# New prices in a kernel's planner, and the low part of a key copied by ScalarE

## The chip, the core and the metric

The kernel runs on one core of a Trainium2 chip. The metric is the device time of one execution in microseconds (us). Names: PE is TensorE (matmuls), PEld its weight loads, DVE is VectorE, ACT is ScalarE, POOL is GpSimd, SP is SyncE, which issues most of the transfers.

## The reference

Two layers of an encoder trunk on x of 512 tokens by 1024, all in float32. Each layer computes

```
u = rms_norm(h)
proj = u @ w_in                        # 1024 x 7424: inputs of three mixers, and gates
a = differential_attention(...)        # 4 heads, two softmax maps each
r = bidirectional_retention(...)       # 4 heads, chunks of 128
c = grouped_query_attention(...)       # 8 query heads, 2 key heads
h = h + (sum over n of gate_n * (branch_n @ w_branch_n)) @ w_out
h = h + relu(rms_norm(h) @ w_mlp_in)**2 @ w_mlp_out      # 1024 -> 4096 -> 1024
```

## The kernel before

**Products.** A float32 operand is held as two tiles: a high part (`w_hi`, `dkh`, `xh`: a copy in the type fp32r, made by ACT) and a low part (`w_lo`, `dkl`, `xl`: the operand minus its high part, made by DVE). A product is three matmuls: high by high, high by low, low by high (`passes`). A matmul writes 128 rows by 512 or 256 columns. Weights come as 512 KB tiles `stage` (two buffers) through SP's queue and are split into `w_hi` and `w_lo` (six buffers). The pairs of MLP and gate units (`pair`, tiles `x`, `c`, `pu`) and the wide MLP products (`wide_product`, tiles `wide`, `A`, `wp`) use Strassen-like schemes: sums and differences on DVE, seven products in place of eight. In a pair, one PSUM tile serves several products in turn, and ACT must copy its content (`c<-x`, `pu<-x`) before the next product may write it.

**Stages of a layer.** Projections and retention come first (`rv`, `rq`, `rk`, `rg`, tiles `rsc`, `rav`), then the differential heads (`diff_head`; `qk` is normalised and rotated by a chain of POOL instructions, `qtr` is its transpose on PE, `dsc` the scores, `dav` the values), the grouped-query heads (`gsc`, `gav`), gates and branch projections, the output product `wo`, and the MLP (`x`, `wide`, `w`).

**The order is planned.** Nothing is issued while the program is written: every instruction goes into a list (`Plan.note`), with the instructions it depends on and a price in ns from `price()`. `Plan.order` then plays the list through: at each moment every idle engine takes, of the instructions whose inputs are ready and whose buffers are free, the one that stands earliest in the program, and is busy for its price. A result reaches another engine after a fixed time (`HOPS`, by pair of engines) plus 200 ns (`HOP`); a transfer through SP has its size by 360 bytes per ns and then 2000 ns. The sequence that comes out is the order in which each engine's instructions are issued. The chip's engines keep that order: an instruction that waits holds up everything behind it on its engine. So a price never changes what is computed, only the places.

Prices before, in ns, with n the columns:

```
matmul, fp32r                 2.5 + n / 2.4
ScalarE                       0.833 * n + 50 (PSUM) or 95
VectorE                       1.04 * n + 69
GpSimd power / other          300 + 165 * n  /  2.1 * n + 130
```

None of them looks at how many of the 128 partitions an instruction covers. Instructions on 64 partitions are those that shift half a tile to the other half: `sw` of `ev_rope_t`, `dq`, `gq`, `dkh`, `dkl`, `gkh`, `gkl` of `stack_q` and `stack_k`, `ctmp` of `gqa_head`.

**A key.** `stack_k` (line 1051) takes the transposed keys of two maps or heads from PSUM. For each of the two it fills all 128 partitions of `hi` and `lo` with the same 64 rows: ACT copies them twice, into their own half and into the other, and DVE subtracts twice. It is called once per differential head and once per layer for the grouped-query keys, each time for two keys: (4 + 1) x 2 x 2 layers = 20 keys.

Of the kernel before, what the change touches and what calls it, by code (L numbers as in the profile page):

```python
# [14 lines left out]
ALU = mybir.AluOpType  # L15
# [233 lines left out]
def free(x):  # L249
    return math.prod(x.shape[1:])  # L250


def price(engine, op, k):

    out = k["out"]
    n = free(out)
    if engine == "tensor":
        if op == "transpose":
            return 112
        if k["rhs"].tile.dtype == F32R:  # L260
            return 2.5 + n / 2.4 * (1 if n >= 256 else 4)
        return 195 if n == 1 else 4 * (2.5 + max(n, 128) / 2.4)
    src = k.get("in_", k.get("in0"))
    if src is not None:
        n = max(n, free(src))
    psum = any(isinstance(x, Ref) and x.tile.psum for x in k.values())
    if engine == "scalar":
        extra = 95 if isinstance(k.get("scale"), Ref) or isinstance(k.get("bias"), Ref) else 0
        return 0.833 * n + (50 if psum else 95) + extra + (100 if "accum_out" in k else 0)
    if engine == "vector":  # L270
        if op == "reciprocal":
            return 65 + 8 * n
        fast = op in ("tensor_scalar", "tensor_copy") and not psum
        pointer = any(isinstance(k.get(x), Ref) for x in ("scalar", "scalar1", "scalar2"))
        return (0.52 if fast else 1.04) * n + 69 + (61 if pointer else 0)
    if engine == "gpsimd":
        if k.get("op") == ALU.pow:
            return 300 + 165 * n
        return (3.4 if op in ("tensor_scalar", "tensor_copy") else 2.1) * n + 130
    return 700  # L280


# [5 lines left out]
class Plan:  # L288
# [16 lines left out]
    def note(self, engine, name, args, kwargs):  # L305
# [22 lines left out]
        for r in ins + outs:  # L328
            if r.tile not in seen:
                seen.append(r.tile)  # L330
                r.tile.users += 1
                if r.tile.first is None:
                    r.tile.first = i
                    o.new.append(r.tile)
        o.tiles = seen
        o.cost = price(engine, name, kwargs) if engine != "sync" else self.dma_price(kwargs)
        o.late = self.LATENCY.get(engine, 0.0)
        if engine == "gpsimd" and name == "dma_start":
# [133 lines left out]
class Core:  # L472
# [578 lines left out]
    def stack_k(self, srcs, nm):  # L1051

        p = self.turned(srcs)
        out = []
        for i in range(2):
            own = slice(i * 64, i * 64 + 64)
            hi, lo = self.g(nm + "h", F32R), self.g(nm + "l", F32R)
            for j in (i, 1 - i):
                self.nc.scalar.copy(out=hi[j * 64:j * 64 + 64], in_=p[own])
            for j in range(2):  # L1060
                self.nc.vector.tensor_tensor(out=lo[j * 64:j * 64 + 64], in0=p[own], in1=hi[own], op=ALU.subtract)
            out.append((hi, lo))
        return out

# [641 lines left out]
```

## Time and profile before

| | |
|---|---|
| median of 3 runs | 1773.45 us (1772.24 to 1774.34) |
| the profiled execution | 1772.2 us, of which its span 1770.4 us |
| busy, share of the span | PE 99%, weight loads 86%, DVE 84%, ACT 64%, POOL 19% |
| instructions | PE 10136, DVE 2438, ACT 2064, POOL 350 |
| granted clock of TensorE | 1.000 |
| moved by DMA | 201.95 MB, mean 114 GB/s |

The span runs from the first to the last instruction; busy time is what the instructions of an engine cover together. The ends of matmuls are modelled, so that the time from one start to the next tells more of PE than its busy share.

### The profile page before, as it was taken

What the parts mean: (1) busy time and instruction counts of PE and PEld (TensorE: products, weight loads), DVE (VectorE), ACT (ScalarE), POOL (GpSimd) and SP (SyncE); (2) the same over time, 40 slices, a digit from 0 to 9 for tenths busy, and PEclk for the clock granted to TensorE, in tenths of its full rate; (3) what the DMA queues carried; (4) which work ended last, traced back from release to release, by engine and by line L of the source; (5) the groups of instructions that cost most, each with busy time, mean ns of one, the idle gap of its engine ahead of it and who ended that gap; (6) DMA issues with size and microseconds to landing.
All of it is one profiled execution on the core that took longest, in us unless ns stands there. A gap on an engine that the chain in (4) does not pass through costs nothing.

```text
span 1770.4 us, 27228 instructions
## 1 busy us (share of the span) xinstructions
PE 1744.6 (99%) x10136; PEld 1525.3 (86%) x10136; DVE 1484.3 (84%) x2438; ACT 1139.0 (64%) x2064; POOL 339.9 (19%) x350
## 2 busy tenths in 40 slices
PE   8999999999999999999999999999999999999999
PEld 6887888889988989988888778888899899989887
DVE  7866887899978999999866667978999789998994
ACT  5544666785556877777535456768855568777771
POOL 2334463001110001111013235700012100011110
PEclk9999999999999999999999999999999999999999
DMA  6311212112355354747622122111124542646482
GB/s 205 106 61 48 86 66 72 48 48 73 115 183 179 96 178 103 219 96 225 206 93 71 48 76 68 60 60 60 36 97 133 160 172 92 211 99 182 96 249 84
DMA packets 76741, 201.95 MB, mean 114 GB/s; under 512 B 8896, under 2 KB 9408, under 8 KB 76608
## 3 DMA queue, kind: packets, MB, share of 16 engines
q1 hardware_dynamic: 68544, 185.53, 32.0%
q0 software_dynamic: 8064, 14.68, 5.6%
q8 instruction: 79, 1.29, 0.3%
q14 instruction: 54, 0.44, 0.1%
HBM read 169.77 MB, written 30.41 MB: 113 GB/s over the span
## 4 chain that ended last, share of the span: by engine, by line
PE 73%; DVE 11%; DMA 6%; ACT 5%; issue 3%; POOL 2%; SPq 0%; ACTq 0%; DVEq 0%; POOLq 0%
PE x L455 19%; PE wide L455 7%; PE proj L455 6%; PE gate L455 6%; DMA stage<-in_w 6%; PE w L455 5%; PE wo L455 5%; PE c L455 4%; DVE w_lo L461 4%; PE wtr L457 2%; PE rg L455 2%; PE gsc L455 2%; PE gav L455 2%; PE dsc L455 2%; PE rq L455 1%
## 5 line engine op out<-in xcount | busy, mean ns | idle before, releaser
L461 ACT CAST w_hi<-stage 128x1024 fp32r<-128x1024 f32 (+1 forms) x235 | 226.8, 968 | 169.0 <-DMA stage<-in_w 95.4
L461 DVE TENSOR_TENSOR w_lo<-stage,w_hi 128x1024 fp32r<-128x1024 f32 (+1 forms) x235 | 282.0, 1202 | 35.1 <-ACT w_hi L461 31.9
L455 PE MATMUL x<-u,w_hi 128*128 128x256 f32 x1472 | 276.1, 283 | 0.0
L455 PEld LDWEIGHTS x<-u,w_hi 128*128 128x128 f32 x1472 | 233.5, 192 | 2.5
L455 PE MATMUL x<-u,w_lo 128*128 128x256 f32 x736 | 208.3, 283 | 0.0
L461 POOL DMA_DIRECT2D sums<-wp x56 | 49.1, 876 | 560.1 <-ACT xh L461 475.2
L455 PEld LDWEIGHTS x<-u,w_lo 128*128 128x128 f32 x736 | 141.1, 192 | 0.0
L455 PE MATMUL wide<-w_lo,xh 128*128 128x512 f32 x336 | 130.9, 390 | 0.0
L455 PE MATMUL wide<-w_hi,xl 128*128 128x512 f32 x336 | 130.8, 389 | 0.0
L455 PE MATMUL wide<-w_hi,xh 128*128 128x512 f32 x336 | 129.7, 390 | 0.0
L461 DVE TENSOR_TENSOR w_lo<-A,w_hi 128x512 fp32r<-128x512 f32 x168 | 112.3, 684 | 10.3 <-ACT w_hi L461 9.5
L455 PE MATMUL x<-t23h,w_hi 128*128 128x256 f32 x368 | 105.2, 287 | 3.3 <-ACT c L461 3.0
L461 ACT CAST w_hi<-A 128x512 fp32r<-128x512 f32 x168 | 102.2, 621 | 8.2 <-ACT w_hi L461 2.7
L455 PE MATMUL gate<-u,w_hi 128*128 128x512 f32 x320 | 106.4, 399 | 0.0
L461 ACT ACTIVATE c<-c 128x512 f32<-128x512 f32 x156 | 94.0, 628 | 19.0 <-DVE c L461 17.3
L455 PE MATMUL x<-t23h,w_lo 128*128 128x256 f32 x368 | 104.3, 283 | 0.3 <-DVE w_lo L461 0.2
L455 PE MATMUL x<-t23l,w_hi 128*128 128x256 f32 x368 | 104.1, 283 | 0.0
L455 PE MATMUL c<-w_hi,u 128*128 128x512 f32 x256 | 86.1, 394 | 0.0
L455 PEld LDWEIGHTS x<-t23h,w_hi 128*128 128x128 f32 x368 | 70.3, 191 | 5.9 <-ACT c L461 5.3
L461 POOL TENSOR_TENSOR gth<-gth,c 128x512 f32<-128x512 f32 x28 | 40.8, 1465 | 178.1 <-DVE c L461 178.0
L455 PEld LDWEIGHTS wide<-w_hi,xl 128*128 128x128 f32 x336 | 63.1, 188 | 13.1
L455 PEld LDWEIGHTS wide<-w_lo,xh 128*128 128x128 f32 x336 | 63.1, 188 | 12.5
(299 smaller groups left out, 5208.9 us busy)
## 6 DMA issues: line engine op xcount, KB each, us to landing
stage<-in_w SPq DMA_DIRECT2D x235, 512.0 KB, 3.6
A<-in_w SPq DMA_DIRECT2D x96, 256.0 KB, 4.6
sums<-wp POOLq DMA_DIRECT2D x56, 256.0 KB, 6.0
sums<-wp SPq DMA_DIRECT2D x28, 256.0 KB, 2.8
wp<-sums SPq DMA_DIRECT2D x28, 256.0 KB, 4.7
h<-in_x SPq DMA_DIRECT2D x16, 256.0 KB, 4.4
mid<-h SPq DMA_DIRECT2D x16, 256.0 KB, 2.1
h<-mid SPq DMA_DIRECT2D x16, 256.0 KB, 6.3
```

The costliest lines, as they stand in the source:

```text
L455: self.nc.tensor.matmul(k.pop("out"), **k)
L457: self.nc.tensor.transpose(k["out"], k["in_"], k["identity"])
L461: getattr(getattr(self.nc, o.engine), o.name)(**k)
```

## The change

The prices of fp32r matmuls, of instructions on fewer than 128 partitions and of GpSimd become larger; and in `stack_k` the second subtraction becomes a copy by ACT of the first one's result.

```diff
         if k["rhs"].tile.dtype == F32R:
-            return 2.5 + n / 2.4 * (1 if n >= 256 else 4)
+            return 13.7 + n / 2.4 * (1 if n >= 256 else 4)
...
     if engine == "scalar":
-        return 0.833 * n + (50 if psum else 95) + extra + (100 if "accum_out" in k else 0)
+        shifted = 115 if out.shape[0] < 128 else 0
+        return 0.833 * n + (50 if psum else 95) + extra + (100 if "accum_out" in k else 0) + shifted
     if engine == "vector":
...
-        return (0.52 if fast else 1.04) * n + 69 + (61 if pointer else 0)
+        return (0.52 if fast else 1.04) * n + 69 + (61 if pointer else 0) + (115 if out.shape[0] < 128 else 0)
     if engine == "gpsimd":
         if k.get("op") == ALU.pow:
-            return 300 + 165 * n
-        return (3.4 if op in ("tensor_scalar", "tensor_copy") else 2.1) * n + 130
+            return 400 + 165 * n
+        return (3.4 if op in ("tensor_scalar", "tensor_copy") else 2.1) * n + 290
...
             hi, lo = self.g(nm + "h", F32R), self.g(nm + "l", F32R)
-            for j in (i, 1 - i):
-                self.nc.scalar.copy(out=hi[j * 64:j * 64 + 64], in_=p[own])
-            for j in range(2):
-                self.nc.vector.tensor_tensor(out=lo[j * 64:j * 64 + 64], in0=p[own], in1=hi[own], op=ALU.subtract)
+            other = slice(64 - i * 64, 128 - i * 64)
+            self.nc.scalar.copy(out=hi[own], in_=p[own])
+            self.nc.scalar.copy(out=hi[other], in_=p[own])
+            self.nc.vector.tensor_tensor(out=lo[own], in0=p[own], in1=hi[own], op=ALU.subtract)
+            self.nc.scalar.copy(out=lo[other], in_=lo[own])
```

The order moves nearly everywhere, by small steps. Three places follow.

PE in the first differential head of layer 1: the score matmuls (`dsc`) among the value projection (`dv`). Before:

```order
L455 MATMUL dsc<-dkh,dq 128x512
L455 MATMUL dv<-w_hi,u_250 128x512
L455 MATMUL dv<-w_lo,u_250 128x512
L455 MATMUL dv<-w_hi,u_278 128x512
L455 MATMUL dsc<-dkh,dq 128x512
L455 MATMUL dv<-w_hi,u_136 128x512
L455 MATMUL dv<-w_lo,u_136 128x512
L455 MATMUL dsc<-dkl,dq 128x512
```

Now:

```order
L456 MATMUL dsc<-dkh,dq 128x512
L456 MATMUL dv<-w_lo,u_146 128x512
L456 MATMUL dv<-w_hi,u_160 128x512
L456 MATMUL dv<-w_hi,u_170 128x512
L456 MATMUL dv<-w_lo,u_170 128x512
L456 MATMUL dv<-w_hi,u_184 128x512
L456 MATMUL dsc<-dkh,dq 128x512
L456 MATMUL dv<-w_hi,u_193 128x512
L456 MATMUL dv<-w_lo,u_193 128x512
L456 MATMUL dv<-w_hi,u_212 128x512
L456 MATMUL dv<-w_hi,u_202 128x512
L456 MATMUL dsc<-dkl,dq 128x512
```

Five projection matmuls now stand between the two that need the high parts, where there were three, and four before the first that needs a low part, where there were two.

DVE in the retention stage of layer 2: the low part of the last chunk's scores (`sdl`) and a weight's low part (`w_lo`). Before:

```order
L461 SCALAR_TENSOR_TENSOR sd<-rsc,decay 128x512 x3
L461 TENSOR_TENSOR sdl<-sd,sdh 128x512 x3
L461 SCALAR_TENSOR_TENSOR sd<-rsc,decay 128x512
L461 TENSOR_TENSOR rot<-rq,t_ret 128x512
L461 TENSOR_SCALAR decay<-delta,dec 128x896
L461 TENSOR_TENSOR w_lo<-stage,w_hi 128x1024
L461 TENSOR_TENSOR sdl<-sd,sdh 128x512
```

Now:

```order
L462 SCALAR_TENSOR_TENSOR sd<-rsc,decay 128x512 x2
L462 TENSOR_TENSOR sdl<-sd,sdh 128x512 x2
L462 SCALAR_TENSOR_TENSOR sd<-rsc,decay 128x512 x2
L462 TENSOR_SCALAR decay<-delta,dec 128x896
L462 TENSOR_TENSOR sdl<-sd,sdh 128x512 x2
L462 SCALAR_TENSOR_TENSOR decay<-delta,dec,decay 128x896
L462 TENSOR_TENSOR rot<-rq,t_ret 128x512
L462 TENSOR_TENSOR w_lo<-stage,w_hi 128x1024
```

The last `sdl` had `rot`, one `decay` instruction and `w_lo` ahead of it; `rot` and `w_lo` now stand behind it.

ACT in the MLP of layer 2, at the end of a wide product: the copies of the wide PSUM tiles (`wp`), the cast of a weight that comes by DMA (`w_hi<-stage`), and the copy `c<-x` that frees a pair's PSUM tile. Before:

```order
L461 COPY wp<-wide_17828 128x512
L461 CAST xh<-c_17437 128x256
L461 CAST xh<-c_17693 128x256
L461 COPY wp<-wide_17843 128x512
L461 CAST w_hi<-stage 128x1024
L461 COPY pu<-x_17886 128x256
L461 COPY c_17933<-x_17907 128x256
```

Now:

```order
L462 COPY wp<-wide_17802 128x512
L462 CAST w_hi<-stage 128x512
L462 CAST w_hi<-stage 128x1024
L462 COPY wp<-wide_17818 128x512
L462 CAST w_hi<-sa 128x1024
L462 COPY wp<-wide_17858 128x512
L462 CAST w_hi<-sb 128x1024
L462 COPY wp<-wide_17876 128x512
L462 COPY pu<-x_17915 128x256
L462 COPY c_17957<-x_17934 128x256
```

The casts of this pair's weights, which stood right ahead of `pu` and `c` or behind them, now stand ahead of three copies of wide tiles.

## Rows read from the trace of the kernel before

**Rows 1.** The page, part 1: busy us, share of the span, instructions.

```profile
PE 1744.6 (99%) x10136; PEld 1525.3 (86%) x10136; DVE 1484.3 (84%) x2438; ACT 1139.0 (64%) x2064; POOL 339.9 (19%) x350
```

**Rows 2.** The chain that ended last, 590 to 640 us: start, length, what.

```profile
610.03 10.07 PE x L455 x84
620.11 10.91 PE wide L455 x48
```

**Rows 3.** Waits of PE's matmuls: us in total, times, longest.

```profile
PE x L455 <- ACT c L461: 5.8, 9, 1.1
PE dsc L455 <- ACT dkh L461: 1.9, 4, 0.6
PE qtr L457 <- POOL qk L461: 1.9, 3, 0.9
PE rav L455 <- DVE sdl L461: 1.7, 1, 1.7
```

**Rows 4.** Waits of PE's weight loads, same columns.

```profile
PEld x L455 <- ACT c L461: 9.6, 17, 1.3
...
PEld dsc L455 <- ACT dkh L461: 4.0, 6, 0.9
PEld dsc L455 <- DVE dkl L461: 3.7, 13, 0.5
PEld qtr L457 <- POOL qk L461: 3.6, 4, 1.3
PEld rav L455 <- DVE sdl L461: 2.1, 1, 2.1
PEld gsc L455 <- ACT gE L461: 1.9, 4, 0.7
PEld dsc L455 <- ACT dE L461: 1.8, 5, 0.4
PEld ms L455 <- ACT gsq L461: 1.5, 4, 1.0
...
PEld ms L455 <- ACT dkh L461: 0.9, 2, 0.4
```

**Rows 5.** Timeline of PE, 1619.5 to 1620.8: start, length, what, idle before.

```profile
1619.57 0.28 PE L455 MATMUL x<-u,w_lo 128*128 128x256 f32 x1
1620.71 0.39 PE L455 MATMUL x<-t23h,w_hi 128*128 128x256 f32 x1 [0.86 <-ACT c L461]
```

**Rows 6.** Tile dkh, ACT and DVE: count, ns (min/median/max), first and last start.

```profile
L461 ACT CAST dkh<-qtr x32: 564/582/587, 159.5 to 1133.0; 64x512 fp32r<-64x512 f32 x32
L461 DVE TENSOR_TENSOR dkl<-qtr,dkh x32: 682/689/696, 161.3 to 1136.2; 64x512 fp32r<-64x512 f32 x32
```

**Rows 7.** The page, part 5, a cast from SBUF: busy us, mean ns, idle before.

```profile
L461 ACT CAST w_hi<-A 128x512 fp32r<-128x512 f32 x168 | 102.2, 621 | 8.2 <-ACT w_hi L461 2.7
```

**Rows 8.** Timeline of ACT near 159 us: start, length, what, count.

```profile
159.47 1.78 ACT L461 CAST dkh<-qtr 64x512 fp32r<-64x512 f32 x3
```

**Rows 9.** Tile w_lo over the whole span, DVE, columns as in rows 6.

```profile
L461 DVE TENSOR_TENSOR w_lo<-stage,w_hi x235: 678/1219/2359, 10.9 to 1740.3; 128x1024 fp32r<-128x1024 f32 x80, 128x512 fp32r<-128x512 f32 x38
```

**Rows 10.** Timeline of DVE near 984 us: start, length, what.

```profile
983.50 1.22 DVE L461 TENSOR_SCALAR decay<-delta,dec 128x896 f32<-128x896 f32 x1
984.64 2.32 DVE L461 TENSOR_TENSOR w_lo<-stage,w_hi 128x1024 fp32r<-128x1024 f32 x1
987.49 1.14 DVE L461 SCALAR_TENSOR_TENSOR decay<-delta,dec,decay 128x896 f32<-128x896 f32 x1
```

**Rows 11.** Timeline of POOL near 984 us, same columns.

```profile
984.32 1.56 POOL L461 TENSOR_TENSOR rot<-rot,sw 128x512 f32<-128x512 f32 x1
```

**Rows 12.** Timeline of ACT near 1619 us, idle time before in brackets.

```profile
1619.06 1.05 ACT L461 CAST w_hi<-stage 128x1024 fp32r<-128x1024 f32 x1 [2.90 <-DMA stage<-in_w]
1620.28 0.38 ACT L461 COPY c<-x 128x256 f32<-128x256 f32 x1
```

**Rows 13.** The chain that ended last, near 1612 us, columns as in rows 2.

```profile
1611.88 7.16 DMA stage<-in_w
```

**Rows 14.** Waits of ACT from 560 to 880 us, columns as in rows 3.

```profile
ACT w_hi L461 <- DMA stage<-in_w: 27.6, 18, 4.6
```

**Rows 15.** Waits of ACT from 1440 to 1770 us, same columns.

```profile
ACT w_hi L461 <- DMA stage<-in_w: 25.2, 12, 3.6
```

## The prediction

> **What bounds the kernel now.** I read the page's busy shares first. PE is at 99%, DVE at 84%, ACT at 64% [rows 1]: whatever the change wins, it wins by letting PE wait less, and work that moves from DVE to ACT counts only where PE waits for it.
>
> Second, the chain that ended last gives PE's pace where nothing holds it: 48 wide matmuls of 512 columns take 10.91 us, so 0.227 each, and 84 of 256 columns take 10.07 us, so 0.120 each [rows 2]. The plan before prices them at 2.5 + 512 / 2.4 = 215.8 ns and 2.5 + 256 / 2.4 = 109.2 ns, 5% and 9% too little; the new 13.7 gives 227.0 and 120.4, what the rows show. So the order before was planned for a PE that runs ahead of the real one.
>
> Third, what PE waits for. The row of the matmuls names ACT's copy `c<-x` (5.8 us), the keys' high parts (1.9), the transposes' inputs from POOL (1.9) and one `sdl` of retention (1.7) [rows 3]. The row of the weight loads shows the same waits longer, and more of them: 9.6, 4.0, 3.6 and 2.1, the keys' low parts with 3.7, and a matmul behind the keys' casts with 0.9 [rows 4]. What PE loses lies between the two. Of one wait it can be read off: matmuls start at 1619.57 and 1620.71 [rows 5], 1.14 us apart where the pace is 0.12, so 1.02 is lost, while the matmul row counts 0.86. The matmul row is too small since the modelled end of a matmul lies behind the moment at which the next could start; the weight loads' row is too large since a load waits while the matmul ahead of it still runs. I take the middle of the two rows, and keep both for the range.
>
> **The change, part by part.**
>
> *Removed and added work.* 20 subtractions of 64 rows leave DVE: 20 x 0.689 = 13.8 us [rows 6]. 20 copies from SBUF come to ACT. No row has one of that height; the nearest are the key's cast from PSUM, 0.582 [rows 6], and a full-height cast from SBUF, 0.621 [rows 7]. I take 0.62, so 12.4 us. Neither engine is the bound, so by itself this is 0. In the chain to a key's second low part, subtraction plus copy (0.69 + 0.62) replaces two subtractions (2 x 0.69): 0.07 us shorter at best. What can cost is ACT's queue: in the first head a full-height `dvh` stands ahead of the two copies. Cover: PE's new order puts four matmuls, 0.9 us, ahead of the first score that needs a low part, where it had two. With that cover gone each of the 20 keys could lose a cast of 0.62, 12 us in all; I take 0.
>
> *A: differential heads.* Here the old prices were wrong in one direction. A 64-row ACT instruction was priced 0.833 x 512 + 50 = 477 ns; three in a row take 1.78 us, 0.59 each [rows 8]. Four key casts and two query casts make a chain, so the plan had it some 0.7 us too short; the POOL chain ahead of the transposes was priced 160 ns too low at each step. So PE was told to take the scores too early. These waits are 4.0 + 3.7 + 3.6 + 0.9 = 12.2 us by the weight loads, 1.9 + 1.9 = 3.8 by the matmuls; the middle is 8.0. In the new order the matmul needing the second high part has five matmuls ahead of it where it had three, so 2 x 0.227 = 0.45 us more cover, and the same shift is in both layers. A wait of the longest kind (0.9) shrinks to half, the shorter ones go. I take three quarters: **-6.0** (bounds -12.2 and 0).
>
> *B: retention.* One `sdl` costs 2.1 by one row and 1.7 by the other, so 1.9. It stood behind a `w_lo` of 2.32 us on DVE [rows 10]; the new order has `w_lo` and `rot` behind it. **-1.9** (bounds -2.1 and 0).
>
> *C: MLP and gate pairs.* PE waits for `c<-x` 9.6 or 5.8 us, the middle 7.7. In the example ACT sat idle 2.90 us for a weight's DMA, cast it, and only then came to `c<-x` [rows 12]. The transfer took 7.16 us [rows 13]; the plan gives it 512 KB / 360 + 2000 ns = 3.5 us, and this price is left alone. What changes is that with PE slower in the plan ACT and DVE run further ahead of it: the cast stands three `wp` copies earlier, and so does the DVE work that frees `stage` for the next transfer. Where the transfer starts earlier too, the wait goes; where it does not, the wait moves ahead of a `wp`. I take half: **-3.9** (bounds -9.6 and the cost in the last rival).
>
> *D: reserve lost.* An order planned for a fast PE left each chain a reserve of 5 to 9%. Waits that were hidden by it come up. The rows of that kind (scores after `gE` and `dE`, norms after `gsq`) hold 1.9 + 1.8 + 1.5 = 5.2 us now [rows 4]. I take a fifth of that again: **+1.0** (bounds 0 and 5.2).
>
> *Sum.* -6.0 - 1.9 - 3.9 + 1.0 = -10.8. The profiled execution took 1772.2 us; it becomes 1761.4. That execution lay 1.25 under the median of the runs, so the median should be **1762.6**. A difference under 0.2%, 3.5 us, is about what a measurement here cannot tell from none.
>
> **The rivals.**
>
> *Only A holds.* The new prices know nothing of instructions that slow each other. `w_lo` takes 1.22 us at the median and up to 2.36 [rows 9], and the one of 2.32 ran beside POOL's `rot`, which took from 984.32 to 985.88 [rows 10, 11]. The `decay` instruction of 1.14 us is of the same kind and still stands near `sdl`; doubled it costs 1.1 us of B's 1.9. With B at -0.8, C at 0 and D at +1.0 the sum is -6.0 - 0.8 + 1.0 = -5.8: median 1767.6. For it: the longest of 235 is twice the median, and prices per instruction cannot show that. Against: the one that cost PE most now stands behind `sdl`.
>
> The Trainium skill (SBUF — State Buffer, section Who interferes with whom) has it as a rule: a DVE instruction with two inputs in SBUF and a GpSimd instruction that reads SBUF exclude each other for a whole instruction. By that rule no price per instruction can plan retention right, and this rival's time follows; rows 9 to 11 agree with it as far as two instructions can.
>
> *No change.* PE is at 99%, and what A wins, D takes: D at its bound of 5.2 and C at 0 give -6.0 - 1.9 + 5.2 = -2.7, median 1770.7, or with A at half +0.3, median 1773.8. For it: after the change the plan's PE has no slack against the real one, while transfers are still planned at half their time. Against: 200 ns for each hop between engines stay in the plan as reserve.
>
> *Slower, by ACT's queue in the MLP.* The casts now ahead of the `wp` copies wait for transfers that the plan believes landed. ACT waits 27.6 us, 18 times, and 25.2 us, 12 times, for them in the two MLP stages [rows 14, 15]. In the example 2.90 us of such waiting cost PE 1.02, a share of 0.35; but over all 52.8 us PE loses only C's 7.7, 0.15, since most waits have no copy behind them that PE needs. If in the new order each has one, 0.35 x 52.8 = 18.5 us are lost, 10.8 more than now; with the transfers no earlier and three copies behind each the share can double, 29 more. With A, B and D this is -6.9 + 10.8 = +3.9 to -6.9 + 29 = +22; I name 1781 as its middle. It decides from a share of 0.28, where the extra loss of 7 us eats A and B. Against it: the DVE work that frees the buffers is earlier as well.
>
> **How the numbers follow.** The forecast (A, B, half of C) gets 0.56, only A 0.19, no change 0.15, slower 0.10. Faster by over 0.2% are the first two: 0.75; within it 0.15; slower 0.10. The predicted time is the forecast's, 1762.6. Its own range is from 1754 (A, B and C near their larger bounds: -10 - 2 - 7) to 1769. The low end stays at 1754; the high end goes to 1772, which takes in the second case and most of the third and leaves out the slower one and little else.
>
> **What would show it.** Right: PE's waits for `dkh`, `dkl` and `qk` under 3 us in the weight loads' row where they are 11.3; no wait of `rav` over 1 us; waits of `x` for `c` at 3 to 6 us in place of 9.6; DVE about 14 us less busy, ACT about 12 more; the pace of 0.227 and 0.120 unchanged. Wrong: waits of `wide` for `wp` of several us, with ACT idle for DMA ahead of them, or scores that wait for `dkl` with an ACT copy as the cause.

## The result: slower, and the profile after

The changed kernel takes 1793.48 us (median; 1789.41 to 1798.44), the kernel before 1773.89 beside it: a ratio of 1.0117 [1.0102, 1.0132], so slower by 1.2% where 0.6% faster was forecast. (This ratio and those below, each with its 95% interval, compare all runs and need not be the quotient of the two medians, which is 1.0110 here.) The profiled execution took 1791.56 us with a span of 1789.8; before, 1772.2 and 1770.4. Lines of the code are numbered one higher than before (L456, L458, L462), and two higher in e5, e6, e11 and e13.

The busy times on the first part of the page of the kernel after moved the way the change says, DVE 16.5 us less than in [rows 1] and ACT 17.1 more, and the counts as it says, 20 fewer and 20 more:

```profile
PE 1749.7 (98%) x10136; PEld 1532.3 (86%) x10136; DVE 1467.8 (82%) x2418; ACT 1156.1 (65%) x2084; POOL 346.3 (19%) x350
```

The waits of the weight loads after (who waits, for what; us in total, times, longest) answer to [rows 4]:

```profile
PEld x L456 <- ACT c L462: 24.3, 18, 5.3
...
PEld x L456 <- ACT pu L462: 3.4, 5, 1.8
PEld rsc L456 <- ACT rkh L462: 3.3, 8, 1.5
PEld gsc L456 <- ACT gE L462: 2.6, 6, 0.5
PEld ms L456 <- ACT gsq L462: 2.5, 6, 1.0
PEld wtr L458 <- DVE dE L462: 2.3, 2, 1.1
...
PEld dsc L456 <- ACT dE L462: 1.9, 6, 0.3
...
PEld dsc L456 <- ACT dkl L462: 0.7, 2, 0.4
...
PEld ms L456 <- ACT dkh L462: 0.6, 2, 0.3
...
PEld dsc L456 <- ACT dkh L462: 0.4, 2, 0.2
```

The waits for a key's parts, for `qk` and for `sdl` are gone or small. Several rows have grown by 3.4 us or less; one has grown by far more: `x` for ACT's `c`, from 9.6 to 24.3 us, and with it the longest wait from 1.3 to 5.3.

**Where that wait comes from.** The chain that ended last, of the kernel after near 1640 us (start, length, what):

```profile
1627.50 7.66 DMA stage<-in_w
...
1635.25 0.06 DVE sa L462
...
1638.48 0.60 DVE c L462
...
1639.60 0.43 DVE c L462
...
1640.11 0.37 ACT c L462
...
1645.06 0.28 ACT c L462
1645.34 0.04 issue
1645.39 4.70 PE x L456 x26
```

And three rows of DVE's and ACT's timelines of the same kernel there (the bracket is the idle time ahead of the instruction):

```profile
1623.23 0.69 DVE L462 TENSOR_TENSOR sa<-stage 128x512 f32<-128x512 f32 x1 [3.15 <-DMA stage<-in_w]
...
1635.25 0.69 DVE L462 TENSOR_TENSOR sa<-stage 128x512 f32<-128x512 f32 x1 [5.18 <-DMA stage<-in_w]
...
1640.11 0.37 ACT L462 COPY c<-x 128x256 f32<-128x256 f32 x1 [4.25 <-DVE c L462]
```

A transfer that the plan takes to last 3.5 us lasts 7.66. DVE has the sum of that tile (`sa<-stage`) next in its order and stands still for 5.18 us, with the sums `c` of an earlier pair behind it. ACT's copy `c<-x` needs the buffer that these sums read, so ACT stands for 4.25; behind the copy come casts and activations, then the next `c<-x`, and PE waits 5.1 us for it. In the trace before, that sum stood behind four more of the `c` sums: of the 32 sums `sa<-stage` of the two MLPs, 12 now have one to four fewer `c` sums ahead of them on DVE, and none has more.

The waits of 2.0 us near the end of either MLP come another way. The chain of the kernel after there in layer 1, and ACT's row:

```profile
825.64 8.80 DMA stage<-in_w
...
834.52 1.04 ACT w_hi L462
835.56 0.28 ACT c L462
```

```profile
834.52 1.04 ACT L462 CAST w_hi<-stage 128x1024 fp32r<-128x1024 f32 x1 [4.57 <-DMA stage<-in_w]
```

Here ACT itself has the cast of a tile under way next in its order, with `c<-x` behind it. In the MLP of layer 2 (1440 to 1780 us, before to 1770) the waits of ACT and DVE of this kind were, before:

```profile
ACT c L461 <- DVE c L461: 6.0, 8, 1.1
...
DVE sa L461 <- DMA stage<-in_w: 5.5, 3, 2.5
```

and after:

```profile
ACT c L462 <- DVE c L462: 15.2, 14, 4.2
...
DVE sa L462 <- DMA stage<-in_w: 12.8, 5, 5.2
```

**A second loss follows it.** Three stretches of the kernel after around that wait (us, busy time of PE, PEld, DVE, ACT, POOL; PEclk is the granted clock as a share of 2.4 GHz; DMA share, GB/s):

```profile
1637.50:1644.50 7.00, 2.78 (x24) 2.58 (x22) 6.80 (x15) 4.33 (x10) 0.00 (x0) 1.00 0.25 73
1645.00:1648.40 3.40, 3.01 (x14) 3.01 (x15) 3.40 (x9) 1.78 (x7) 0.00 (x0) 0.50 0.01 2
1648.50:1655.00 6.50, 6.50 (x47) 6.09 (x46) 5.18 (x8) 4.68 (x9) 0.00 (x0) 1.00 0.25 85
```

After the wait the clock is at the lower of its two levels, 1.2 GHz, and the matmuls there start 0.21 us apart where the pace is 0.12. Within the span of the kernel after, its end left out, there are five such stretches of 3.41 us, 17.1 us together. By the trace 73 matmuls of 256 columns start in them, 0.213 us apart in place of 0.120, a loss of some 7 us; in the profiled execution of before there is none.

**The account.** Take every step from one matmul's start to the next and subtract the pace (0.227, 0.120 and 0.110 us for 512, 256 and 128 columns, 0.112 for a single one); the sum is what PE lost, the half clock included. "Attention" is from `rv` to the first gate matmul, "gate" from there to `wo`, which takes in the grouped-query heads and the gate pairs, both layers together. The last column is the time spent at half clock:

| profiled execution | attention | gate | `wo` and MLP | all | at half clock |
|---|---|---|---|---|---|
| before | 20.3 | 6.6 | 10.9 | 37.9 | 0 |
| after | 13.0 | 12.2 | 32.1 | 57.3 | 17.1 |

The sum grows by 19.4 us, as the span does: attention won 7.3, the gate stage lost 5.6 and `wo` with the MLP 21.2, together 26.8. Within the gate stage the part up to the first pair went from 4.8 to 4.1, and the pairs from 1.8 to 8.3.

### The profile page after: what moved, and what is told of

It reads as the page before. It is cut to its first block, busy times and chain, and to the rows that moved or that the text cites. A ratio compares the mean times of both kernels' runs of the same rounds, so it can differ in the third digit from the quotient of the medians.

```text
span 1789.8 us, 27301 instructions
## 1 busy us (share of the span) xinstructions
PE 1749.7 (98%) x10136; PEld 1532.3 (86%) x10136; DVE 1467.8 (82%) x2418; ACT 1156.1 (65%) x2084; POOL 346.3 (19%) x350
## 3 DMA queue, kind: packets, MB, share of 16 engines
q1 hardware_dynamic: 68544, 185.53, 31.4%
## 4 chain that ended last, share of the span: by engine, by line
PE 66%; DVE 18%; DMA 5%; ACT 4%; issue 2%; POOL 0%; DVEq 0%; ACTq 0%; SPq 0%; POOLq 0%
PE x L456 14%; DVE w_lo L462 6%; PE wide L456 5%; PE c L456 5%; PE w L456 5%; PE wo L456 5%; PE gate L456 5%; DMA stage<-in_w 5%; PE proj L456 5%; PE dv L456 2%; DVE c L462 2%; PE wtr L458 2%; PE rg L456 2%; ACT w_hi L462 2%; PE dsc L456 2%
## 5 line engine op out<-in xcount | busy, mean ns | idle before, releaser
L462 ACT CAST w_hi<-stage 128x1024 fp32r<-128x1024 f32 (+1 forms) x235 | 226.3, 967 | 178.9 <-DMA stage<-in_w 60.5
L462 DVE TENSOR_TENSOR w_lo<-stage,w_hi 128x1024 fp32r<-128x1024 f32 (+1 forms) x235 | 273.5, 1169 | 49.5 <-ACT w_hi L462 48.5
L456 PE MATMUL x<-u,w_hi 128*128 128x256 f32 x1472 | 278.6, 286 | 3.5 <-ACT pu L462 2.5
L456 PEld LDWEIGHTS x<-u,w_hi 128*128 128x128 f32 x1472 | 235.1, 194 | 8.5 <-ACT pu L462 3.4
L456 PE MATMUL x<-u,w_lo 128*128 128x256 f32 x736 | 209.3, 285 | 0.0
L462 POOL DMA_DIRECT2D sums<-wp x56 | 49.0, 886 | 572.8 <-ACT wp L462 447.8
L456 PEld LDWEIGHTS x<-u,w_lo 128*128 128x128 f32 x736 | 142.5, 194 | 0.0
L456 PE MATMUL wide<-w_hi,xh 128*128 128x512 f32 x336 | 130.9, 390 | 0.0
L456 PE MATMUL wide<-w_lo,xh 128*128 128x512 f32 x336 | 130.9, 390 | 0.0
L456 PE MATMUL wide<-w_hi,xl 128*128 128x512 f32 x336 | 130.7, 389 | 0.0
L456 PE MATMUL x<-t23h,w_hi 128*128 128x256 f32 x368 | 106.9, 291 | 15.0 <-ACT c L462 15.0
L462 ACT CAST w_hi<-A 128x512 fp32r<-128x512 f32 x168 | 103.3, 622 | 21.5 <-PE x L456 14.0
L462 DVE TENSOR_TENSOR w_lo<-A,w_hi 128x512 fp32r<-128x512 f32 x168 | 112.3, 680 | 3.0 <-ACT w_hi L462 3.0
L456 PE MATMUL gate<-u,w_hi 128*128 128x512 f32 x320 | 106.1, 400 | 0.0
L456 PE MATMUL x<-t23l,w_hi 128*128 128x256 f32 x368 | 105.8, 288 | 0.3
L456 PE MATMUL x<-t23h,w_lo 128*128 128x256 f32 x368 | 105.6, 287 | 0.0
L462 ACT ACTIVATE c<-c 128x512 f32<-128x512 f32 x156 | 95.1, 628 | 9.4 <-DVE c L462 7.3
L456 PEld LDWEIGHTS x<-t23h,w_hi 128*128 128x128 f32 x368 | 71.5, 195 | 17.4 <-ACT c L462 17.4
L456 PE MATMUL c<-w_hi,u 128*128 128x512 f32 x256 | 85.8, 395 | 0.0
L462 ACT COPY c<-x 128x256 f32<-128x256 f32 x138 | 51.0, 370 | 44.3 <-DVE c L462 23.1
L462 ACT CAST w_hi<-sa 128x1024 fp32r<-128x1024 f32 x46 | 48.3, 1051 | 47.9 <-DVE sa L462 33.0
L462 POOL TENSOR_TENSOR gth<-gth,c 128x512 f32<-128x512 f32 x28 | 42.0, 1507 | 188.6 <-DVE c L462 188.6
```

The costliest lines, as they stand in the source:

```text
L456: self.nc.tensor.matmul(k.pop("out"), **k)
L462: getattr(getattr(self.nc, o.engine), o.name)(**k)
```

## The experiments

Ratios are to runs of the kernel before on the same chip in the same batch; losses are of the profiled execution, counted as above.

| run | median, us | ratio [95%] | attention | gate | `wo`, MLP | half clock |
|---|---|---|---|---|---|---|
| e1 | 1822.53 | 1.0296 [1.0277, 1.0315] | 31.4 | 19.7 | 32.6 | 27.3 |
| e2 | 1774.37 | 1.0016 [1.0002, 1.0030] | 19.4 | 9.5 | 14.0 | 10.2 |
| e3 | 1779.14 | 1.0038 [1.0024, 1.0051] | 23.3 | 11.1 | 9.5 | 0 |
| e4 | 1785.83 | 1.0079 [1.0064, 1.0094] | 24.0 | 6.9 | 21.5 | 20.5 |
| e5 | 1769.67 | 0.9991 [0.9975, 1.0007] | 13.5 | 7.0 | 22.3 | 3.4 |
| e6 | 1800.74 | 1.0163 [1.0140, 1.0186] | 18.0 | 11.5 | 36.7 | 37.5 |
| e7 | 1798.58 | 1.0155 [1.0133, 1.0176] | 15.4 | 14.0 | 35.1 | 27.3 |
| e8 | 1808.08 | 1.0209 [1.0182, 1.0235] | 31.3 | 18.0 | 22.4 | 20.5 |
| e9 | 1779.32 | 1.0030 [1.0017, 1.0044] | 14.4 | 12.6 | 19.8 | 13.7 |
| e10 | 1788.93 | 1.0083 [1.0055, 1.0112] | 13.8 | 12.7 | 28.6 | 13.7 |
| e11 | 1782.12 | 1.0046 [1.0030, 1.0062] | 13.8 | 6.8 | 24.5 | 6.8 |
| e12 | 1766.05 | 0.9960 [0.9945, 0.9974] | 13.8 | 12.5 | 4.2 | 0 |
| e13 | 1769.22 | 0.9976 [0.9966, 0.9986] | 13.4 | 7.5 | 15.6 | 6.8 |
| e14 | 1759.46 | 0.9924 [0.9911, 0.9936] | 12.9 | 6.8 | 5.8 | 0 |
| e15 | 1765.98 | 0.9961 [0.9947, 0.9974] | 17.7 | 9.8 | 5.0 | 0 |

### Which part of the change costs

**e1, the matmul price alone.** The kernel before with one line of the change:

```diff
-            return 2.5 + n / 2.4 * (1 if n >= 256 else 4)
+            return 13.7 + n / 2.4 * (1 if n >= 256 else 4)
```

> The kernel before with nothing but the new price of matmuls (13.7 in place of 2.5). Theory 1, the matmul price alone brings DVE's and ACT's work on weights that are still under way by DMA ahead of the pair's PSUM copies in the MLP: this has all of the loss and none of the gain in the differential heads that the other prices bring, so 1790 to 1800 us, waits of x for c (weight loads) 20 to 28 us as in the changed kernel. Theory 2, the higher prices of half-height and GpSimd work or the copy moved to ACT make the loss: within 4 us of 1774, waits of x for c about 10 us.

**e2, all but the matmul price.** The changed kernel with that line undone.

> The changed kernel with the matmul price put back to 2.5; half-height and GpSimd prices and the copied key stay. Theory 1: the MLP has its old order, waits of x for c are back at 8 to 11 us, the differential heads keep their gain, so 1764 to 1770 us, faster than before. Theory 2: 1785 to 1795 us, as slow as the changed kernel.

**e3, the key's copy alone**, under the prices of before (the last hunk of the change).

> The kernel before with the key's second low part copied by ACT, all prices old. Theory 1: no loss and little gain, 1771 to 1776 us; DVE about 14 us less busy and ACT about 12 more. Theory 2: if the copy on ACT is what costs, 1780 us or more with waits of the scores for dkl that grow.

Measured: the matmul price carries the loss, and alone it is worse than the whole change. None of the three times fell in a window: e1 lies 22 us above theory 1's, with that theory's waits of `x` for `c` (25.4 us); e2 and e3 lie between the two windows each. Without the new matmul price the loss is gone (e2), but so is the gain that was expected there: attention keeps 19.4 of before's 20.3 us, and `x` waits 14.0 us for `c` where 8 to 11 were expected. In e1 the attention heads lose 11 us more than before, too. Its weight loads' waits:

```profile
PEld x L455 <- ACT c L461: 25.4, 16, 5.1
...
PEld gsc L455 <- ACT gE L461: 5.8, 12, 0.8
PEld dsc L455 <- DVE dkl L461: 5.5, 12, 1.0
PEld qtr L457 <- POOL qk L461: 4.3, 6, 1.1
```

So a true price of PE with the other engines still priced too low uncovers their chains; the half-height and GpSimd prices are what turns that into a gain (e7 below, which has all the prices and not the copy, loses 15.4 in attention). The copy under the old prices costs 0.4% (e3), though not by theory 2's sign: its scores wait 0.3 us for the copied `dkl`.

### Where the matmul price costs

**e4, longer transfers in the plan, everywhere.**

```diff
-    LATENCY = {"sync": 2000.0}
+    LATENCY = {"sync": 4000.0}
```

> The changed kernel with the plan's latency of SP's transfers raised from 2000 to 4000 ns, so that a weight tile is planned at 5.5 us in place of 3.5 (the traces show 5.8 to 8.8 us where PE was held). Theory 1 with the transfer price as its root: the casts and DVE's first sums of a new tile go back behind the pair's copies in part, waits of x for c fall under 12 us from 24.3, total 1762 to 1778 us. If the transfers are not the root but only the truer pace of PE is: 1785 us or more still.

The waits of `x` for `c` fell to 2.4 us, as the theory has it, but the time missed its window by 8 us and lies in the other one, of 1785 us or more: with every transfer planned late, attention lost 11 us more than after, and the MLP kept 21.5. So this run by itself does not decide; e9 and e12 do.

**e5 and e6, the price split by place.** The changed kernel with

```diff
-            return 13.7 + n / 2.4 * (1 if n >= 256 else 4)
+            mlp = out.tile.name.startswith(("x", "wide", "w2"))
+            return (2.5 if mlp else 13.7) + n / 2.4 * (1 if n >= 256 else 4)
```

and, for e6, 2.5 and 13.7 exchanged.

> The changed kernel, with the old matmul price (2.5) for the matmuls that write x, wide and w2 (gate pairs and MLP) and 13.7 for all others. The order in the MLP is then that of before. Theory 1 (the loss comes from the MLP's order alone, the price helps the attention heads): the stages from the first retention product to the first gate lose 13 us of PE time as in the changed kernel, where before lost 20, the others lose before's 18; no stretches at half clock; 1764 to 1770 us. Theory 2 (a true matmul price takes reserve from every stage, wherever it is set): waits of dsc, rsc, wtr and ms come up, 1774 to 1785 us.

> The counterpart: the changed kernel with 13.7 for x, wide and w2 alone and 2.5 for all other matmuls. Theory 1: gate pairs and MLP lose as in the changed kernel, with waits of x for ACT's c of 20 us and more and 10 us or more at half clock; the attention heads as in the run with all but the matmul price, 6 us worse than the changed kernel: 1793 to 1803 us. Theory 2 (reserve in every stage): half of the loss stays, 1780 to 1788 us.

Both times fell where theory 1 put them. With the old price in pairs and MLP the time is that of before or just below, with it elsewhere it is worse than the whole change. Attention in e5 loses 13.5 us, as after. (The profiled execution of e5 was the slowest of its ten, 1776.86; its 22.3 in the MLP, 3.4 us of it at half clock where theory 1 had none, belong to that execution, 7 us above the median, and the others lost less there. At the median, too, e5 is only 1.7 us faster than before though attention gains 6.8, so some 5 us are still lost elsewhere: an estimate, and no trace of a median execution shows where.)

**e7, without the key's copy**: the changed kernel with the two subtractions back.

> The changed kernel with all its prices, but the key's second low part subtracted by DVE as before. Theory 1 (the copy does not matter where the plan has the prices right): waits of x for c as in the changed kernel, 1790 to 1796 us. Rival a (ACT's queue is fuller by 17 us and that holds the copies of x): 1783 to 1788. Rival b (the copy is what takes away the waits for dkl): waits of dsc for dkl of 3 us or more, 1796 to 1801.

The time is in rival b's window, but its sign is missing: waits of `dsc` for `dkl` are 1.2 us. What rose are waits of `dsc` for `dE` (7.1 us, 14 times, from 1.9) and the half clock, 27.3 from 17.1 us. By the ratios the copy gains 0.4% under the new prices (1.0155 without it, 1.0117 with it) and costs 0.4% under the old ones; why was not settled.

**e8, more allowance for each hop**: `HOP = 400.0` in the changed kernel.

> The changed kernel with the plan's allowance for each hop between engines at 400 ns in place of 200. In the MLP the casts and sums of transfers stay as early as in the changed kernel. Theory 1 (transfers planned too short hold ACT and DVE): waits of x for c of 15 us or more, 1785 to 1798 us. Theory 2 (the reserve that the short matmul price gave is what is missing): the waits on POOL and DVE chains (gsc, wtr, ms, rb) fall, and those of x for c to under 10: 1768 to 1780 us.

Outside every window, and theory 1's sign, 15 us or more of waits of `x` for `c`, is missing too. The waits of `x` moved from `c` (8.3 us) to `pu` (9.5), and new ones came up in attention: `gsc` for `gE` 5.8, `rav` for `sdl` 5.4, `rb` for `rs` 4.8. A flat reserve on every hop doesn't replace what was lost; theory 2 of that run falls by its time.

### The transfers priced

**e9 and e10, the MLP's weight transfers alone**, at 6000 and 8000 ns of latency:

```diff
...
-        o.late = self.LATENCY.get(engine, 0.0)
+        o.late = 6000.0 if self.mlp else self.LATENCY.get(engine, 0.0)
...
+        self.nc.mlp = PLAN[q % NQ][0][0] in ("w1", "w2")
         self.nc.sync.dma_start(out=t, in_=self.a["w"][q])
+        self.nc.mlp = False
```

> The changed kernel, true matmul price everywhere, but the plan's latency of the w1 and w2 transfers to a stage tile set from 2000 to 6000 ns (7.5 us with the transfer itself); all other transfers stay at 2000. The casts of MLP transfers come back to where before has them, the sums to 2 us of matmuls ahead of it. Theory 1 (the loss is a transfer planned too short, which a true PE price uncovers): waits of x for ACT's c under 8 us, no wait over 3, 1766 to 1776 us. Rival (what a true price takes away is reserve on DVE and ACT in the MLP, whatever the transfers): waits of x for c, of w for w_lo and of rb for msr add to 15 us or more, 1780 to 1792 us.

> The same with 8000 (9.5 us with the transfer). Casts stand 1.7 us, sums 3.8 us of matmuls later than before has them. Theory 1: as with 6000 or better, 1764 to 1776 us. Rival: weights now come late by plan, PE waits for w_lo and w_hi in the MLP, 1778 to 1795 us.

e9 wins back 14 of the 20 us and misses its window by 3, and the sign too: `x` still waits 17.1 us for `c`, up to 5.6. What is left in its MLP is above all two waits of PE, 5.6 and 5.0 us, one per layer. The chain that ended last of e9, at the first of them:

```profile
813.81 11.60 DMA wp<-sums
...
827.25 0.70 DVE wp L462
827.95 0.02 issue
827.97 0.72 ACT wp L462
828.69 0.27 ACT c L462
828.96 0.04 issue
829.00 1.01 PE x L456 x3
```

It is the same figure with another transfer: `wp<-sums`, which reads back the sums of the wide products, takes 11.6 us where the plan has 2.7 (256 KB / 360 + 2000 ns). DVE's sums of `wp`, ACT's scaling of them and the copy `c<-x` queue up behind it. The stretches of e9 ahead of the wait's end and behind it show the clock:

```profile
819.00:828.00 9.00, 4.57 (x39) 4.36 (x37) 3.25 (x6) 2.34 (x5) 0.00 (x0) 1.00 1.02 316
829.00:835.00 6.00, 6.00 (x28) 6.00 (x29) 6.00 (x10) 2.09 (x2) 0.00 (x0) 0.50 0.40 127
```

In e10, which fell in its rival's window, the weights are late by plan: `x` waits for `w_lo` 7.2 us and for `w_hi` 3.7. So 8000 ns is worse here than 6000.

**e11, the old price in pairs and MLP with 4000 ns for these transfers.**

> The run with the old matmul price in gate pairs and MLP, and the latency of the MLP's transfers at 4000 ns in place of 2000. Theory 1: waits of x for c, 18 us there, fall to under 8: 1758 to 1768 us, faster than before. Rival (reserve is used up on the other side: weights come later than PE wants them): waits of x for w_lo or w_hi over 5 us, 1770 to 1785 us.

Theory 1 fails here and the rival's window and sign hold: waits for `c` did fall to 2.1, but `x` waits for `w_lo`:

```profile
PEld x L457 <- DVE w_lo L463: 10.0, 5, 3.9
```

The likely reason, which no run tests by itself: with the short matmul price the plan's PE runs ahead, which already puts the casts late, and a later transfer on top is too much. In the MLP the two short prices of before were covering each other: corrected alone, each makes the kernel slower (the matmul price in the kernel after and e6, the transfers in e11 against e5), while with the new matmul price the longer transfers win time (e9, e12).

**e12, both transfers priced**: e9 with 10000 ns for `wp<-sums` (`mlp` now holds the latency itself); and **e13**, the old price in pairs and MLP with the same 10000 ns, the weight transfers at 2000.

```diff
...
+            nc.mlp = 10000.0
             nc.sync.dma_start(out=x, in_=self.sums[n, s])
+            nc.mlp = False
```

> The run with the MLP's weight transfers at 6000 ns, and the latency of the transfers wp<-sums set from 2000 to 10000 ns as well (10.7 us with the transfer). Theory 1 (every wait of ACT or DVE for a transfer planned too short holds the copies that PE needs): the two waits of 5.6 and 5.0 us go, and with them two stretches of 6.8 us at half clock, 3.4 lost in each: 1779 - 10.6 - 6.8 = 1762, so 1758 to 1767 us, faster than before. Rival (the wait moves to the next thing that ACT or DVE has in its queue): a wait of x, turn or w of 3 us or more in each MLP, 1770 to 1780 us.

> The run with the old matmul price in gate pairs and MLP (2000 ns for the weight transfers), with the latency of wp<-sums at 10000 ns. Theory 1: that order had no long wait behind wp<-sums, so the time stays, 1766 to 1773 us, and the run with both transfers priced is faster than this one. Rival (the short price in the MLP is as good as true prices): equal within 3 us.

e12 came in its window, faster than before. The MLP's loss falls from 32.1 us (after) to 4.2, under before's 10.9. The weight loads' waits of e12, and its clock (span, mean granted clock):

```profile
PEld x L456 <- ACT c L462: 6.2, 10, 1.1
```

```profile
core 0: 1762.9 us, clock 1.000
```

e13 also came in its window, and is 3.2 us slower than e12; their intervals overlap a little, and the two differ in the gate pairs as well. e14 below has e13's short price in the gate pairs and differs from it in the MLP alone, in the matmul price and the 6000 ns for the weights; its interval, 0.9911 to 0.9936, lies clear of e13's, 0.9966 to 0.9986. So in the MLP the new matmul price together with the longer transfers is the faster pair.

**e14 and e15, the gate pairs**, whose stage in e12 still loses 12.5 us where before it lost 6.6. e14 is e12 with 2.5 for the gate pairs' matmuls alone; e15 is e12 with 4000 ns for the gate weights' transfers.

> The run with both transfers priced, but 2.5 in place of 13.7 for the matmuls of the gate pairs (named gx here), still 13.7 in the MLP. Theory 1 (in gate pairs too the true price uncovers something else that the plan has too short): the gate stage loses 7 us of PE time in place of 12.5, 1758 to 1763 us. Rival (the gate stage's losses come from the other prices, GpSimd's above all): 12 us stay, 1764 to 1768.

> The run with both transfers priced, true matmul prices everywhere, and the gate weights' transfers at 4000 ns in place of 2000 (5.5 with the transfer). Theory 1a (the same cause as in the MLP, transfers): the gate stage loses 8 us or less, 1758 to 1763. Theory 1b (there it is DVE's sums of a stage tile, which take 1.4 to 1.8 us beside GpSimd in place of 0.69, and no price of transfers helps): 11 us or more stay, 1764 to 1769.

e14 is the fastest version: 0.9924, 12 us under before and 34 under the changed kernel. With the other prices of e12, the gate pairs do better under the short price than under the new one. Pricing the gate weights' transfers (e15) took 2.7 us from the gate's loss, between the two marks, and attention lost 3.9 more; its time lies in theory 1b's window. But e4, with the new matmul price and 4000 ns for all of SP's transfers, has 6.9 in the gate column, as before has. So the new price need not cost there; which of the other transfers it takes, no run separates. One wait there is not behind a transfer at all. DVE's rows of e12 ahead of a wait of 1.05 us:

```profile
423.14 1.41 DVE L462 TENSOR_TENSOR sb<-stage 128x512 f32<-128x512 f32 x1
424.48 1.77 DVE L462 TENSOR_TENSOR sa<-sa,stage 128x512 f32<-128x512 f32 x1
426.18 0.68 DVE L462 TENSOR_TENSOR w_lo<-stage,w_hi 128x512 fp32r<-128x512 f32 x1
```

and POOL's row of e12 at the same time:

```profile
422.71 3.00 POOL L462 TENSOR_TENSOR gth<-gth,c 128x512 f32<-128x512 f32 x2 [20.50 <-DVE c L462]
```

A sum of that size takes 0.69 us alone (the row at 1635.25 above) and 1.41 and 1.77 beside GpSimd. The Trainium skill (SBUF — State Buffer, section Who interferes with whom) has the rule that a DVE instruction with two inputs in SBUF and a GpSimd instruction that reads SBUF exclude each other; these rows agree. Whether this is what the short price covers in the gate pairs was not tried by itself.

## Why the prediction was wrong

*Work removed and added*, counted at 0: right in the sign of the busy times (13.8 us off DVE and 12.4 onto ACT were counted, 16.5 and 17.1 measured over the whole change), and no score waits more than 0.4 us for the copied low part. But the copy's worth for the time was not 0: the changed kernel is 0.4% slower without it (e7), and the old one 0.4% slower with it (e3).

*A, differential heads, -6.0*: held. The four kinds of waits, 12.2 us by the weight loads in [rows 4], are 1.7 after, and from the first `c` to the first gate PE loses 6.6 us where it lost 12.7, whatever came up there included.

*B, retention, -1.9*: held; no wait of `rav` for `sdl` is left. The longest instruction of [rows 10] really stood behind it.

*D, reserve lost, +1.0*: right in kind, low in size. The three waits named, 5.2 us, are 7.0, and others came up beside them (`rsc` for `rkh`, 0.9 before, is 3.3; `wtr` for `dE`, in no row before, is 2.3). A, B and D together were forecast at -6.9, and attention shows -7.3.

*C, MLP and gate pairs, -3.9*: this step failed. It read the right wait, the right transfer (7.16 against 3.5, [rows 13]), and then let "further ahead" be good: where the transfer starts earlier the wait goes. In the plan it is ready 3.5 us after its issue wherever that lies. What the true price changed is what stands behind the wait: casts and sums of the transferred tile moved ahead of work that PE needed. Where -3.9 was forecast, the gate stage and the MLP lose 26.8 us more; some 7 of that is the half clock, which no step had. For the 21.2 of `wo` and MLP, e9 and e12 show the transfers as the cause. For the 5.6 of the gate stage the cause stays open: e14 shows that the matmul price brings it, and no run what it uncovers there.

*The rivals "only A holds" and "no change"*: neither came. B's wait went in full and the waits that D named grew by only 1.8 us; both had C at 0 at worst.

*The rival "slower"* had this mechanism in kind and gave C a cost of 10.8 to 29 us. That 26.8 lies inside is in part luck, since the half clock and the gate stage are in it and were not in that sum. Its +3.9 to +22 has its middle at 1786.4 and not at the 1781 named, and its 0.10 was far too low. Its place was narrow: it looked at casts on ACT ahead of `wp` copies. The longest waits go through DVE's queue, `sa<-stage`, and only then reach ACT; those of 2.0 us do stand behind a cast on ACT, but ahead of `c`; the waits of `wide` for `wp` that were to show it never came. The argument against it, that the work on DVE which frees the buffers is earlier as well, failed since DVE itself stood waiting for transfers: it lost 3.15 us at 1623.23 to the one before, and only after that tile's sums and `w_lo` was the buffer free for the transfer that started at 1627.50.

With these two transfers planned near the longest times seen, the change takes 1766.05 in e12, and 1759.46 in e14 with the old price in the gate pairs besides. Both lie in the range that was forecast for the change without that, which does not make the forecast right: it left the transfers' price alone.

## What to carry to other kernels

In an order made by a planner, prices that are wrong together can hold each other up, as here: with the one that was measured best corrected, the next too-short one, a transfer, became the wait. Before correcting a price, list what else in the same stage the plan has too short, and ask what will stand behind that wait in an engine's queue once the order moves. Price a transfer where it runs, not by one number for all: 4000 ns everywhere cost attention what it saved in the MLP.

## What was not expected of the hardware

A wait of PE can cost more than its length. In the kernel after, the granted clock was 0.50 for 3.41 us behind waits of some 2 to 5 us in the MLP, and in e9 for 6.83 us behind those of 5.6 and 5.0; the start-to-start time of 256-column matmuls was 0.213 us there in place of 0.120. In e12, whose waits after the first weights are 1.2 us at most, the clock stayed at 1.000. The length of one wait does not decide it: before, the clock stayed at 1.000 after the wait of 1.9 us for `sdl`, and in e2 it fell to 0.50 for 3.41 us at 259.6 us, behind two waits of 0.9 and 0.7 us (counted as in the account) at 255 and 258. What does decide was not tried.

And transfers of one kind differ widely within one execution. The median times from issue to landing, of the kernel after and of e9 (operation, count, size, us):

```profile
stage<-in_w SPq DMA_DIRECT2D x235, 512.0 KB, 3.5
```

```profile
wp<-sums SPq DMA_DIRECT2D x28, 256.0 KB, 5.5
```

Single weight tiles in the MLP of the kernel after took 7.66 and 8.80 us, and a single read back of e9 11.60.
